# The last projection of a gated mixer layer by seven products over pairs of chunks

## The chip, the cores and the metric

The kernel runs on one core of a Trainium2 chip. The metric is the time of one execution on the device in microseconds (us). A time from a profile belongs to one profiled execution, in which every instruction has a start and a duration. The engines have these names: PE is TensorE (its weight loads are listed apart as PEld), DVE is VectorE, ACT is ScalarE, POOL is GpSimd, and SP is SyncE, which issues the DMA transfers here. PE writes its sums to PSUM, where DVE and ACT read them; everything else lies in SBUF or in the chip's memory.

## What is computed

One layer of a streaming encoder, in f32, with a sequence of 2048 rows and 1024 channels:

```python
h = rms_norm(x, norm_g[l]) * (1.0 + scale) + shift
u = h @ w_in[l]
glu_in, gate_a, q, k, v, gate_b, m_a, m_b = jnp.split(u, IN_SPLITS, axis=-1)
y_a = conformer_conv_branch(glu_in, gate_a, w_dw[l], b_dw[l], ln_g[l], ln_b[l], w_conv_out[l])
...
o = stick_breaking_attention(q, k, v).reshape(bsz, seq, D_SB)
y_b = (o * jax.nn.silu(gate_b)) @ w_sb_out[l]
y = jax.nn.sigmoid(m_a) * y_a + jax.nn.sigmoid(m_b) * y_b
x = x + gate * (y @ w_out[l])
```

The convolution branch is a gated linear unit, a causal depthwise convolution of width 31 and a layer norm. The change concerns the last line, `y @ w_out`, a product of 2048 x 1024 by 1024 x 1024.

## The kernel before

The arrays lie transposed, with 128 channels on the partitions. The sequence is cut into four chunks of 512 rows (`CH`, `NCH`), and a matrix with 1024 channels into eight tiles of 128 x 512 (`KC` = 8; `JC` = 4 for the 512 channels of a branch). Every f32 operand is split in two: `hi` is a rounded copy (by ACT's cast, L102) and `lo` is what is left of it (a subtraction, L103). A product of f32 quality is then three matmuls into one PSUM tile, hi·hi, hi·lo and lo·hi (`mm3`, L135); all matmuls are recorded under L115, so groups are told apart by the names of their tiles. `dense` (L140) runs `mm3` over eight blocks of channels: 24 matmuls of 128x512 for one output tile.

The stages follow one another:

- To 167 us: modulation vectors, the norm, `h` in all four chunks, and the first group of q.
- To about 620 us, the **convolution stage**. Its code runs through blocks one after another: `glu(j)` (L645; two pieces of weights, B and A), `silu_block` (the gates `ga` and `gb`), `qk_group` and `v_block` (two pieces each). A **piece** is a 128x1024 block of weights, loaded by `piece(src)` in two halves: SP loads a half into a tile `wl` (two buffers), ACT casts it to `whi`, POOL subtracts to get `wlo`. The pieces rotate through three slots, two in the pool `wpa` and one in `wpb`, which every third piece takes. Most blocks are four groups of 24 matmuls. Beside them DVE runs the taps of the convolution (L620), which `tick()` hands out at a fixed rate, and reads the sums of PE out of PSUM (five buffers). ACT computes sigmoids and squares. POOL does little but L103.
- To about 790 us: the layer norm of the convolution branch, with group 5 of v and some gates as matmuls beside it. It begins when the convolution's results (`cv`) are stored and read back.
- To about 1540 us: attention by heads, with the matmuls of the merge gates `ma` and `mb` as filler.
- The **last stage**: for each chunk, `y_tiles` (L1036) forms eight tiles of `y` from the branches' operands `za` (convolution) and `zb` (attention output times its gate, which POOL multiplies at L1030), and then `out_tile` (L1065) forms eight tiles of the projection. The results of `y_tiles` are split into `yh` (ACT, L1061) and `yl` (DVE, L1062). The output weights `wo0` to `wo7` are loaded and split once at the start of this stage and stay; `wo0` lies in the left pool `wr`, the others in the right pool `wor`. One output tile is evicted by one DVE instruction (L1073), gate times sum plus x, and stored.

Each engine works through its instructions in a fixed order. In the convolution stage the order is that of the code (the pin at the stage's start), with the taps put late by a priority; in the last stage it comes from the program's order and from when tiles come free. SP issues loads and stores in one order, too, so that a load can stand behind a store that waits for its data.

The core of the last stage:

```python
for ch in range(NCH):
    ...
    for _ in ygen:
        pass
    if ch + 1 < NCH:
        za = load_za(ch + 1)
        zb = load_zb(ch + 1)
    for j in range(KC):
        ...
        out_tile(ch, j, y, psum)
```

## Time and profile before

| what | us |
|---|---|
| runs | 1875.19 (median), 1873.1, 1876.87 |
| the profiled execution | 1877.81 |
| its span, first to last instruction | 1876.1 |
| PE busy in the span | 1797.0 |
| last matmul starts | 1871.44 |

The page gives each engine's busy time, the span in 40 slices (each 46.9 us; a digit is the busy share in tenths) and the chain of work that ended last, followed back from the end. A row of a group reads: line, engine, operation, output<-inputs, shape and count, then busy time, mean of one in ns, and the idle time of the engine just before them with what ended it. A row of windows reads: stretch, its length, the busy time of PE, PEld, DVE, ACT and POOL with counts, then the granted clock of PE, the busy share of the DMA engines, and GB/s.

### The profile page before, as it was taken

The page shows a single profiled execution, that of the slowest core. Times are in us where ns is not written, and L with a number is a line of the kernel's source. Part 1 is how long each engine was busy: PE and PEld are TensorE (multiplying, and loading weights), DVE is VectorE, ACT ScalarE, POOL GpSimd, SP SyncE. Part 2 cuts the span into 40 slices and gives each one's busy share as a digit, 9 for nine tenths or more (in the row PEclk, how much of TensorE's full clock was granted, in tenths as well). Part 3 has the DMA queues.
Part 4 walks back from the last instruction along what each step waited for, and adds up shares of the span by engine and source line. Part 5 has one row for each costly group of instructions (what it writes and reads, how often), then busy time and mean ns, then how long its engine had stood idle before and what let it go on. Part 6 is the DMA issues. An engine that isn't in the chain of part 4 may idle for free.

```text
span 1876.1 us, 27226 instructions
## 1 busy us (share of the span) xinstructions
PE 1797.0 (96%) x9612; PEld 1517.0 (81%) x9612; DVE 1228.2 (65%) x1696; ACT 812.8 (43%) x1880; POOL 681.3 (36%) x899
## 2 busy tenths in 40 slices
PE   6899999999999998999999999999999899999999
PEld 5888889899888977778877778777788677888887
DVE  7646578888879354467777777777777895334341
ACT  5465113232231122267766777776777752010110
POOL 0343111111121143466666666666666641010100
PEclk9999999999999999999999999999999999999999
DMA  8553402325132443432232323132322446353532
GB/s 288 169 186 105 137 29 80 90 67 148 45 104 93 157 141 118 149 128 81 79 96 68 102 63 109 61 93 70 99 65 88 131 143 215 107 163 96 164 95 79
DMA packets 117596, 211.08 MB, mean 113 GB/s; under 512 B 15442, under 2 KB 27730, under 8 KB 117460
## 3 DMA queue, kind: packets, MB, share of 16 engines
q1 hardware_dynamic: 116308, 207.24, 35.5%
q10 hardware_dynamic: 1152, 2.10, 0.3%
q8 instruction: 76, 1.25, 0.3%
q14 instruction: 60, 0.49, 0.1%
HBM read 137.98 MB, written 71.30 MB: 112 GB/s over the span
## 4 chain that ended last, share of the span: by engine, by line
PE 72%; DVE 8%; POOL 6%; issue 5%; DMA 5%; ACT 4%; SPq 1%; DVEq 0%; ACTq 0%; POOLq 0%
PE pd L115 38%; PE po L115 9%; PE p L115 8%; PE av L115 5%; PE pT L120 5%; PE z L115 5%; POOL w L952 3%; DVE sc L945 2%; POOL wlo L103 1%; ACT z L941 1%; DMA xt<-in_x_n_dram 1%; PE pt L120 1%; DVE tlo L979 1%; DMA wa<-in_w_ada_dram 1%; DMA gt<-ga 1%
## 5 line engine op out<-in xcount | busy, mean ns | idle before, releaser
L952 POOL TENSOR_TENSOR w<-w,sc 128x512 f32<-128x512 f32 (+1 forms) x320 | 361.6, 1130 | 251.8 <-DVE sc L945 179.1
L115 PE MATMUL pd<-hhi,whi 128*128 128x512 f32 x1024 | 413.4, 404 | 1.0 <-ACT vsg L858 1.0
L115 PE MATMUL pd<-hhi,wlo 128*128 128x512 f32 x1024 | 402.7, 393 | 0.0
L115 PE MATMUL pd<-hlo,whi 128*128 128x512 f32 x1024 | 402.5, 393 | 0.0
L945 DVE TENSOR_TENSOR_SCAN sc<-z,sc,w 128x512 f32<-128x512 f32 x192 | 245.0, 1280 | 90.9 <-ACT z L941 83.6
L103 POOL TENSOR_TENSOR wlo<-wl,whi 128x512 fp32r<-128x512 f32 x88 | 131.3, 1503 | 401.4 <-ACT whi L102 401.2
L115 PEld LDWEIGHTS pd<-hhi,wlo 128*128 128x128 f32 x1024 | 193.5, 189 | 42.5 <-POOL wlo L103 0.2
L940 ACT ACTIVATE w<-z 128x512 f32<-128x512 f32 (+1 forms) x320 | 172.2, 538 | 125.7 <-PE z L115 100.0
L115 PEld LDWEIGHTS pd<-hhi,whi 128*128 128x128 f32 x1024 | 195.5, 191 | 35.4 <-ACT vsg L858 1.4
L115 PEld LDWEIGHTS pd<-hlo,whi 128*128 128x128 f32 x1024 | 194.3, 190 | 34.3
L979 DVE TENSOR_TENSOR tlo<-pT,thi 128x512 fp32r<-128x512 f32 (+1 forms) x320 | 184.2, 598 | 35.8 <-ACT thi L978 32.4
L115 PE MATMUL z<-kt,q 128*128 128x512 f32 (+2 forms) x640 | 192.7, 382 | 5.0 <-DVE sc L945 3.5
L978 ACT CAST thi<-pT 128x512 fp32r<-128x512 f32 (+1 forms) x320 | 165.4, 527 | 61.3 <-PE pT L120 57.4
L120 PE MATMUL pT<-ident,w 128*128 128x128 f32 x1088 | 173.1, 275 | 9.8 <-POOL w L952 9.5
L120 PEld LDWEIGHTS pT<-ident,w 128*128 128x128 f32 x1088 | 137.5, 141 | 45.9 <-POOL w L952 14.5
L115 PE MATMUL pd<-whi,hhi 128*128 128x256 f32 x608 | 169.7, 287 | 3.6 <-ACT hhi L131 1.9
L941 ACT ACTIVATE z<-z 128x512 f32<-128x512 f32 (+1 forms) x320 | 171.7, 537 | 0.0
L115 PE MATMUL pd<-whi,hlo 128*128 128x256 f32 x608 | 167.0, 285 | 2.3 <-DVE hlo L131 1.7
L115 PE MATMUL pd<-wlo,hhi 128*128 128x256 f32 x608 | 154.0, 284 | 0.0
L949 DVE TENSOR_TENSOR_SCAN sc<-z,tri 128x512 f32<-128x512 f32 (+3 forms) x128 | 104.4, 819 | 53.9 <-ACT z L941 41.9
L115 PE MATMUL av<-tlo,vt 128*128 128x512 f32 (+1 forms) x320 | 123.2, 385 | 14.0 <-DVE tlo L979 10.9
L115 PEld LDWEIGHTS z<-kt,q 128*128 128x128 f32 x640 | 109.6, 189 | 24.1 <-DVE sc L945 5.4
(284 smaller groups left out, 3108.4 us busy)
## 6 DMA issues: line engine op xcount, KB each, us to landing
wl<-in_w_in_dram SPq DMA_DIRECT2D x64, 256.0 KB, 2.9
wa<-in_w_ada_dram SPq DMA_DIRECT2D x24, 512.0 KB, 5.1
wl<-in_w_qkv_dram SPq DMA_DIRECT2D x36, 256.0 KB, 2.7
xt<-in_x_n_dram SPq DMA_DIRECT2D x16, 512.0 KB, 5.5
vst<-st SPq DMA_DIRECT2D x64, 128.0 KB, 2.0
kt<-kst SPq DMA_DIRECT2D x32, 256.0 KB, 2.8
vt<-vst SPq DMA_DIRECT2D x32, 256.0 KB, 2.7
q<-qst SPq DMA_DIRECT2D x32, 256.0 KB, 2.8
```

Of the source, the lines that this page charges most:

```text
L103: (lo_eng or nc.gpsimd).tensor_tensor(out=lo[:, s], in0=wl, in1=f(hi[:, s]), op=ALU.subtract)
L115: i = nc.tensor.matmul(*a, **k)
L120: i = nc.tensor.transpose(*a)
L940: nc.scalar.activation(out=w[:, lo:], in_=z[:, lo:], func=AF.Sigmoid, scale=HD ** -0.5)
L941: nc.scalar.activation(out=z[:, lo:], in_=z[:, lo:], func=AF.Sigmoid, scale=-HD ** -0.5)
L945: nc.vector.tensor_tensor_scan(out=s[:, 1:], data0=z, data1=w, initial=s[:, 0:1], op0=ALU.mult, op1=ALU.bypass)
L949: nc.vector.tensor_tensor_scan(out=s[:, lo + 1:], data0=z[:, lo:], data1=tri[:, :CH - lo], initial=1.0, op0=ALU.mult, op1=ALU.max)
L952: nc.gpsimd.tensor_tensor(out=w[:, lo:], in0=w[:, lo:], in1=s[:, lo:CH], op=ALU.mult)
L978: nc.scalar.copy(out=thi[:, :n], in_=pT[:, :n])
L979: nc.vector.tensor_tensor(out=tlo[:, :n], in0=pT[:, :n], in1=f(thi[:, :n]), op=ALU.subtract)
```

## The change

Two chunks are taken together. With y cut in two halves of channels and two chunks, and `w_out` in two by two halves, the projection of a pair is a product of 2 x 2 blocks, which Strassen's method forms with seven block products instead of eight; each has weights A, operands B and one or more outputs, which are sums and differences of blocks. The table `SEVEN` lists for each product its terms of A, of B and its outputs as (row, column, sign), in the order in which they run: 2, 4, 1, 6, 3, 7, 5. A block product is 4 output tiles of 4 blocks of channels, 48 matmuls; there are 14 in all.

- **The weights' sums.** `prepare()` stands in the convolution stage behind each `piece` of `glu` and `silu_block`, 14 times. Each call makes two of the 28 sums (seven products by four j): loads of one or two 128x512 blocks into `wl`, POOL's addition where there are two terms, the cast, POOL's subtraction, and two stores to the chip's memory (`ws`). It takes a slot of `wpa` or `wpb` and counts as a piece in their rotation. Products 2, 1, 6, 7 and 5 have two terms, 4 and 3 one.
- **The products.** `operands` loads the four weights of a product (512 KB each) and forms its B: POOL's sum where there are two terms, ACT's cast, DVE's subtraction. It is called one product ahead. `product` runs the matmuls, and DVE adds each PSUM tile, times gate or minus gate, to one or two accumulators per output tile (`acc`, twelve buffers, loaded with x); the last addition is followed by the store. The operands go by turns to tiles `za`, `zb` and `oa`, `ob`; `ob` lies in the right pool `yr`, the other three left.
- **The order.** The y tiles of chunks 0 and 1 run one after the other, then seven products, then the y tiles of chunks 2 and 3, then seven products. y stays in f32, so the split behind `y_tiles` goes, and so do the resident output weights. The buffers of `io` go from four to eight.

```diff
+    SEVEN = {
+        2: (((1, 0, 1), (1, 1, 1)), ((0, 0, 1),), ((1, 0, 1), (1, 1, -1))),
+        4: (((1, 1, 1),), ((1, 0, 1), (0, 0, -1)), ((0, 0, 1), (1, 0, 1))),
+        1: (((0, 0, 1), (1, 1, 1)), ((0, 0, 1), (1, 1, 1)), ((0, 0, 1), (1, 1, 1))),
...
+        5: (((0, 0, 1), (0, 1, 1)), ((1, 1, 1),), ((0, 0, -1), (0, 1, 1))),
+    }
+    LASTS = {(1, 0): 4, (1, 1): 3, (0, 0): 5, (0, 1): 5}
+    H = KC // 2
...
+        def prepare():
+
+            npiece[0] += 1
+            pool = wpb if npiece[0] % 3 == 0 else wpa
+            hi = pool.tile([P, 1024], F32R, tag="whi", name="whi")
+            lo = pool.tile([P, 1024], F32R, tag="wlo", name="wlo")
+            for i in range(2):
+                m, j = wanted.pop(0)
+                s = slice(i * CH, (i + 1) * CH)
+                w = []
+                for r, c_, _ in SEVEN[m][0]:
+                    w.append(wpa.tile([P, CH], F32, tag="wl", name="wl", bufs=2))
+                    nc.sync.dma_start(w[-1], w_out[j + H * r][:, c_ * CH:(c_ + 1) * CH])
+                if len(w) == 2:
+                    nc.gpsimd.tensor_tensor(
+                        out=w[0], in0=w[0], in1=w[1],
+                        op=ALU.add if SEVEN[m][0][1][2] > 0 else ALU.subtract)
+                nc.scalar.copy(out=hi[:, s], in_=w[0])
+                nc.gpsimd.tensor_tensor(out=lo[:, s], in0=w[0], in1=f(hi[:, s]),
+                                        op=ALU.subtract)
+                ws_d[m, j] = dram(f"ws{m}_{j}", [P, 2, CH], F32)
+                nc.sync.dma_start(ws_d[m, j][:, 0, :], f(hi[:, s]))
+                nc.sync.dma_start(ws_d[m, j][:, 1, :], f(lo[:, s]))
...
                 w = piece(w_in[B_GLU_B + j])
+                prepare()
                 for g in ORDER:
...
-            return yp.tile([P, CH], F32, tag="io", name=name, bufs=4)
+            return yp.tile([P, CH], F32, tag="io", name=name, bufs=8)
...
+        def operand(q, half, i):
+
+            pool = yr if (q, half) == ("o", "b") else yp
+            return pool.tile([P, 2, CH], F32R, tag=f"{q}{half}{i}", name=f"{q}{half}{i}")
...
-                nc.vector.tensor_tensor(out=ma, in0=ma, in1=mb, op=ALU.add)
-                hi = yp.tile([P, CH], F32R, tag=f"yh{j}", name=f"yh{j}")
-                lo = yp.tile([P, CH], F32R, tag=f"yl{j}", name=f"yl{j}")
-                nc.scalar.copy(out=hi, in_=ma)
-                nc.vector.tensor_tensor(out=lo, in0=ma, in1=f(hi), op=ALU.subtract)
...
+                y[ch, j] = (yr if ch % 2 else yp).tile([P, CH], F32, tag=f"y{j}", name=f"y{j}")
+                nc.vector.tensor_tensor(out=y[ch, j], in0=ma, in1=mb, op=ALU.add)
                 yield
...
+        def operands(m, ch):
+
+            q = "zo"[turn[0] % 2]
+            turn[0] += 1
+            A, B = [], []
+            for j in range(H):
+                A.append(operand(q, "a", j))
+                nc.sync.dma_start(f(A[j]), ws_d[m, j])
+            for kc in range(H):
+                B.append(operand(q, "b", kc))
+                t = combined(SEVEN[m][1], lambda t: y[ch + t[1], kc + H * t[0]],
+                             lambda: yp.tile([P, CH], F32, tag="io", name="sum", bufs=8),
+                             nc.gpsimd)
+                nc.scalar.copy(out=B[kc][:, 0, :], in_=t)
+                nc.vector.tensor_tensor(out=B[kc][:, 1, :], in0=t, in1=f(B[kc][:, 0, :]),
+                                        op=ALU.subtract)
+            return A, B
...
+        def product(m, ch, A, B, psum):
+            for j in range(H):
+                ps = psum("po")
+                for kc in range(H):
+                    s = slice(kc * P, (kc + 1) * P)
+                    mm3(ps, A[j][:, 0, s], A[j][:, 1, s], B[kc][:, 0, :], B[kc][:, 1, :],
+                        kc == 0, kc == H - 1)
+                for r, c_, sign in SEVEN[m][2]:
...
+                    nc.vector.scalar_tensor_tensor(
+                        out=o, in0=ps, scalar=(gate if sign > 0 else ngate)[:, row:row + 1],
+                        in1=o, op0=ALU.mult, op1=ALU.add)
+                    if LASTS[r, c_] == m:
+                        nc.sync.dma_start(out_t[row][:, ts_], o)
...
+        za, zb = load_za(1), load_zb(1)
+        steps(ygen)
+        steps(y_tiles(1, za, zb, psum, y))
+        ya = s3.enter_context(tc.tile_pool(name="ya", reuse_waits="tile", bufs=1, side="right"))
+        for ch in (0, 2):
             if ch:
...
+                za3, zb3 = load_za(3), load_zb(3)
+                steps(y_tiles(2, za, zb, psum, y))
+                steps(y_tiles(3, za3, zb3, psum, y))
+            order = list(SEVEN)
+            nxt = operands(order[0], ch)
+            for i, m in enumerate(order):
+                A, B = nxt
+                if i + 1 < len(order):
+                    nxt = operands(order[i + 1], ch)
+                elif ch == 0:
+                    za, zb = load_za(2), load_zb(2)
+                product(m, ch, A, B, psum)
```

Two places show how the instructions move. The first is POOL in the convolution stage, from the second piece of `glu(2)` to the two pieces of `qk_group(2)` and of `v_block(4)`. Before, only the real pieces' subtractions stand there (two per piece; the numbers tell the pieces apart):

```order
L103 TENSOR_TENSOR wlo_3866<-wl_3867,whi_3865 128x512
L103 TENSOR_TENSOR wlo_3866<-wl_3871,whi_3865 128x512
L103 TENSOR_TENSOR wlo_3992<-wl_3993,whi_3991 128x512
L103 TENSOR_TENSOR wlo_3992<-wl_3997,whi_3991 128x512
L103 TENSOR_TENSOR wlo_4002<-wl_4003,whi_4001 128x512
L103 TENSOR_TENSOR wlo_4002<-wl_4007,whi_4001 128x512
```

After the change, on the same engine at the same place, with the additions of `prepare` at L234 and its subtractions at L238:

```order
L103 TENSOR_TENSOR wlo_4008<-wl_4009,whi_4007 128x512
L103 TENSOR_TENSOR wlo_4008<-wl_4013,whi_4007 128x512
L234 TENSOR_TENSOR wl_4019<-wl_4019,wl_4021 128x512
L238 TENSOR_TENSOR wlo_4018<-wl_4019,whi_4017 128x512
L234 TENSOR_TENSOR wl_4029<-wl_4029,wl_4031 128x512
L238 TENSOR_TENSOR wlo_4018<-wl_4029,whi_4017 128x512
L103 TENSOR_TENSOR wlo_4156<-wl_4157,whi_4155 128x512
L103 TENSOR_TENSOR wlo_4156<-wl_4161,whi_4155 128x512
L103 TENSOR_TENSOR wlo_4166<-wl_4167,whi_4165 128x512
L103 TENSOR_TENSOR wlo_4166<-wl_4171,whi_4165 128x512
```

Four POOL instructions, each pair behind loads of its own, now stand ahead of the two pieces 4156 and 4166 of `qk_group(2)`.

The second place is DVE where y tiles begin behind a projection. Before, at the end of chunk 1's projection and the start of chunk 2's y tiles, the splits of the next operands (L1010) stand ahead of most of the projection's evictions (L1073):

```order
L1010 TENSOR_TENSOR zb_17167<-o,zb_17167 128x512
L1010 TENSOR_TENSOR zb_17175<-o,zb_17175 128x512
L1073 SCALAR_TENSOR_TENSOR xt<-po,gate,xt 128x512
L1010 TENSOR_TENSOR zb_17183<-o,zb_17183 128x512
L1073 SCALAR_TENSOR_TENSOR xt<-po,gate,xt 128x512 x7
L1056 TENSOR_TENSOR ma<-p_17427,ma 128x512
```

After, where the seventh product of the first pair ends (evictions at L1160) and chunk 2's y tiles begin (their first reading of PSUM at L1108); `za_177..` and `zb_177..` are operands of chunk 3:

```order
L1057 TENSOR_TENSOR za_17770<-n,za_17770 128x512
L1057 TENSOR_TENSOR zb_17780<-o,zb_17780 128x512
L1057 TENSOR_TENSOR zb_17788<-o,zb_17788 128x512
L1160 SCALAR_TENSOR_TENSOR acc<-po,ngate,acc 128x512
L1160 SCALAR_TENSOR_TENSOR acc<-po,gate,acc 128x512
L1057 TENSOR_TENSOR za_17775<-n,za_17775 128x512
L1057 TENSOR_TENSOR zb_17796<-o,zb_17796 128x512
L1057 TENSOR_TENSOR zb_17804<-o,zb_17804 128x512
L1108 TENSOR_TENSOR ma<-p_17816,ma 128x512
L1109 TENSOR_TENSOR mb<-p_17829,mb 128x512
```

Three splits of chunk 3 now stand between the last eviction of the product and the first of chunk 2's y tiles, where nothing stood between projection and y tiles before.

More of the change, by code (lines that the diff above doesn't have):

```diff
@@ L1014, in load_za @@
             for kc in range(JC):
-                t = yp.tile([P, 2, CH], F32R, tag=f"za{kc}", name=f"za{kc}")
+                t = operand("zooz"[ch], "a", kc)
                 o = io("n")
@@ L1024, in load_zb @@
             for kc in range(JC):
-                t = yp.tile([P, 2, CH], F32R, tag=f"zb{kc}", name=f"zb{kc}")
+                t = operand("zooz"[ch], "b", kc)
                 o = io("o")
@@ new lines, in y_tiles, with combined @@
+                nc.vector.tensor_tensor(out=y[ch, j], in0=ma, in1=mb, op=ALU.add)
+                yield
+        def combined(terms, part, tmp, eng):
+            if len(terms) == 1:
+                return part(terms[0])
+            t = tmp()
+            (a, b) = terms
+            eng.tensor_tensor(out=t, in0=part(a), in1=part(b),
+                              op=ALU.add if b[2] > 0 else ALU.subtract)
+            return t
+        turn = [0]
+        def operands(m, ch):
[14 more added lines that the diff above has]
+            return A, B
```

50 lines of the change are left out of this document (22 added, 28 removed), and 3 rows, old and new, of the table SEVEN.

## The prediction

> **What bounds the kernel now.** I read the page first (busy shares, slices, the chain's shares), then the chain of waits in order of time, then windows by stage.
>
> ```profile
> PE 1797.0 (96%) x9612; PEld 1517.0 (81%) x9612; DVE 1228.2 (65%) x1696; ACT 812.8 (43%) x1880; POOL 681.3 (36%) x899
> DVE  7646578888879354467777777777777895334341
> PE 72%; DVE 8%; POOL 6%; issue 5%; DMA 5%; ACT 4%; SPq 1%; DVEq 0%; ACTq 0%; POOLq 0%
> ```
>
> TensorE is busy 96% of the span and holds 72% of the chain. The VectorE slices fall to 1 to 4 tenths in the last eighth, so an added operation is cheap there, and stand at 7 and 8 in slices 4 to 12, where the weights are to be prepared.
>
> ```profile
> 167.87 5.47 PE pd L115 x24
> ...
> 191.51 115.86 PE pd L115 x624
> ...
> 621.34 2.51 POOL wlo L103 x2
> ...
> 1567.41 39.93 PE po L115 x170
> 1607.33 43.52 PE p L115 x192
> 1650.86 44.64 PE po L115 x192
> ...
> 1827.19 44.66 PE po L115 x192
> ```
>
> Start, length and count of pieces of the chain. From 191 us the convolution stage is pure TensorE; its first gap is at 621. The tail alternates y tiles (`p`) and output projection (`po`) with nothing between. So a matmul removed from the tail is time, and so is any gap added to the convolution stage: a late piece of weights has no cover.
>
> **Tail: the matmuls.** 4 x 8 x 8 x 3 = 768 become 2 x 7 x 4 x 4 x 3 = 672.
>
> ```profile
> L115 PE MATMUL po<-yh,wo7l 128*128 128x512 f32 x32 | 12.7, 396 | 0.0
> L115 PE MATMUL po<-yh,wo0l 128*128 128x512 f32 x32 | 12.5, 390 | 0.0
> L115 PE MATMUL p<-za,wc2l 128*128 128x512 f32 x16 | 6.3, 391 | 0.0
> ```
>
> A `po` piece takes 44.64/192 = 0.2325 us per matmul, a `p` piece 43.52/192 = 0.2267. The modelled means say which operand matters: wo0, in the left pool as the y weights are, reads like `p` (390 ns), wo7 in the right pool 396. The products' weights all lie in the left pool, but in every second product the moving operand `ob` lies right, where no row shows it. Four pieces make 178.6 us; 672 matmuls cost 152.3 at 0.2267, 156.2 at 0.2325. Gain 22.4 to 26.3; I take the middle, **-24.5**, as half the operands are of the unseen kind.
>
> **Tail: the other engines.**
>
> ```profile
> L1073 DVE SCALAR_TENSOR_TENSOR xt<-po,gate,xt 128x512 f32<-128x512 f32 x32 | 23.7, 750 | 100.2 <-PE po L115 92.0 <-DMA xt<-in_x_t_dram 8.2
> L1062 DVE TENSOR_TENSOR yl<-ma,yh 128x512 fp32r<-128x512 f32 x32 | 22.1, 691 | 19.8 <-ACT yh L1061 19.6
> L1030 POOL TENSOR_TENSOR o<-o,gb 128x512 f32<-128x512 f32 x13 | 17.0, 1313 | 201.6 <-DMA gb<-gb 125.5 <-DMA o<-o 76.1
> L1010 DVE TENSOR_TENSOR zb<-o,zb 128x512 fp32r<-128x512 f32 x13 | 13.9, 1067 | 20.9 <-ACT zb L1009 20.4
> ```
>
> 96 evictions replace 32: 64 x 0.75 = 48 us of VectorE; 56 splits replace 32: 24 x 0.69 = 17. A product of 48 matmuls (10.9 us) holds about 7 evictions (5.2) and 4 splits (2.8), so VectorE fits, and so do 4 POOL sums of 1.31. Cost 0 inside the products. At the end two evictions stand behind the last matmul where one stood: **+0.75**.
>
> ```profile
> 1565.15 0.39 PE L115 MATMUL po<-yh,wo0l 128*128 128x512 f32 x1
> 1566.60 0.51 PE L115 MATMUL po<-yh,wo0h 128*128 128x512 f32 x1 [1.06 <-ACT yh L1061]
> 1567.41 0.50 PE L115 MATMUL po<-yl,wo0h 128*128 128x512 f32 x1 [0.30 <-DVE yl L1062]
> ```
>
> These gaps (starts 1.45 and 0.81 apart instead of 0.225) are waits for the y split, which goes: **-1.8**. In its place chunk 1's y tiles stand directly behind chunk 0's, and wait for their gated attention operand: load, POOL product, cast, split. One such chain is 2.7 + 1.31 + 0.62 + 1.07 = 5.7 us; bounds 0 and 5.7, and I take what the gap there is today, **+1.8**. At chunk 2, VectorE has chunk 3's splits (za, zb) ahead of chunk 2's first evictions, as the rows of the change show; while they wait for loads, evictions and with them PSUM stand still. Bounds 0 and one chain again: **+3**.
>
> ```profile
> 1566.00:1571.00 5.00, 4.10 (x16) 3.11 (x17) 3.19 (x5) 2.93 (x6) 0.00 (x0) 1.00 0.95 311
> ```
>
> Transfers in the first pair's products: 28 weight loads of 512 KB, 16 x_t loads, 16 stores, 12 z loads of 256 KB are 26 MB, of which some 5 are issued ahead: 21 MB in 76 us is 280 GB/s. This window moved 311 at a DMA share of 0.95, so it fits, tightly. Bounds 0 and 8 (26 MB at 311 GB/s take 84 us): **+1**.
>
> **Convolution stage: what the preparation costs.** Each of 14 calls adds two sums behind a piece of weights; 10 calls have two terms in each sum, 4 have one. All go through the same two `wl` buffers and three piece slots as the real pieces, and through POOL in program order.
>
> ```profile
> L102 ACT CAST whi<-wl x48: 607/620/657, 166.0 to 599.9; 128x512 fp32r<-128x512 f32 x48
> L103 POOL TENSOR_TENSOR wlo<-wl,whi x48: 1285/1307/2336, 166.7 to 600.8; 128x512 fp32r<-128x512 f32 x48
> ...
> DMA to landing us min/median/max: 2.5/2.7/4.3
> ...
> L103 POOL TENSOR_TENSOR wlo<-wl,whi 128x512 fp32r<-128x512 f32 x49 | 80.6, 1658 | 365.7 <-ACT whi L102 365.5
> ```
>
> The first three are the tile `wl` from 160 to 620 us (ns, min/median/max), the last the group's mean there. A POOL pass takes p = 1.31 us alone and up to 2.34; the mean, 1.66, is what I use.
>
> ```profile
> 599.59 3.53 POOL L103 TENSOR_TENSOR wlo<-wl,whi 128x512 fp32r<-128x512 f32 x2 [18.22 <-ACT whi L102]
> ...
> 600.65 1.32 DVE L620 SCALAR_TENSOR_TENSOR cc<-v,wsum,cc 128x1024 f32<-128x1024 f32 x1
> 601.89 2.31 DVE L620 SCALAR_TENSOR_TENSOR cb<-u,wdw,cb 128x1024 f32<-128x1024 f32 x1
> ...
> 336.00:358.00 22.00, 22.00 (x101) 18.23 (x100) 22.00 (x19) 5.67 (x7) 3.88 (x2) 1.00 0.35 96
> ```
>
> Two passes beside convolution taps take 3.53 together and the tap among them 2.31 where the one before took 1.32: they take turns. In the window 336 to 358 VectorE is busy all 22 us.
>
> The chain for a sum of two terms is load 2.7, add p, cast 0.62, subtract p: 3.32 + 2p = 6.6. Two sums, then the real piece (load, cast, two subtractions; its first load is partly under the sum before): 9.96 + 6p = 19.9, against a block of 4 x 5.47 = 21.9. So a call is hidden behind its block on the mean, with 2 us to spare; scatter of p up to 2.34 costs some. Seven calls stand so: 7 x 0.5 = **+3.5** (0 at p = 1.31; 7 x 1.9 = 13 at 2.3).
>
> Three calls (before qk1, qk2 and v5) stand ahead of **two** pieces, which are used at once, 1.4 us apart: 13.28 + 8p = 26.6 against 23.3, 3.3 late each: **+9.8** (1.4 at 1.31, 25 at 2.3). The second piece of a pair now takes the slot that the block just before it frees; cast and subtraction behind that are within these 3.3.
>
> What the added waits hold up: on SP a sum's two stores wait for its POOL subtraction, and behind them stand the next `wl` loads, which is in the chain above, and stores of gate and q tiles, at most one sum late. On ScalarE 28 casts (17 us) wait for loads ahead of the sigmoids that free PSUM; ScalarE is busy 5.67 of 22 us in the window above and five PSUM buffers stand ahead: 0, and up to one chain of 6.6 if PSUM fills. The 27 MB of added loads and stores in 450 us are 60 GB/s beside 96 at a share of 0.35: 0.
>
> ```profile
> 666.53 1.39 PE L115 MATMUL psb<-dg,ones 128*128 128x128 f32 x8 [2.38 <-DVE dg L755]
> ...
> 667.25:670.66 3.41, 3.41 (x11) 2.78 (x10) 2.80 (x5) 0.98 (x2) 1.91 (x3) 0.50 0.45 148
> ```
>
> After an idle time of 2.38 us the granted clock was 0.50 for 3.41 us: half of those, 1.7, were lost. Stalls of 3.3 would do the same: 3 x 1.7 = **+5.1** (0 to 5.1). [...]
>
> Removed from the attention stage's end: 16 casts, 16 VectorE subtractions and 16 loads of the output weights; there TensorE was the bound and they cost nothing, nor does their going gain.
>
> **Sum** against the profiled execution (1877.81; span 1876.1, and 1.7 around it): -24.5 + 0.75 - 1.8 + 1.8 + 3 + 1 + 3.5 + 9.8 + 5.1 = -1.35. The profiled run lies 2.6 above the median of the runs; carried to that, 1875.19 - 1.35 = 1873.8.
>
> **Rivals.**
> *The preparation is hidden.* With p near its median 1.31 the pairs lose 1.4, the rest and the clock nothing: 17 less, about **1856.8**. For it: the median, and stretches such as 415 to 460 in which taps pause. Against it: POOL passes come in rows here, and the second of a row pays.
>
> *POOL and the taps take turns, slower than before.* Added POOL passes make rows of four to eight behind each other while taps stream. At p = 2.1 the pairs cost 20.3, the seven others 4.6, the clock 5.1: 30.0 instead of 18.4, **1885.4**; at 2.3, 1898. It decides from p = 1.72 (no gain) and from 1.87 (slower by 0.2%). For it: the 3.53 us pair and VectorE's full windows; delayed taps also come late at 620, where the LN stage waits. Against it: TensorE's own stalls give VectorE time to pause. [...]
>
> *Transfers bind the products.* 26 MB at 311 GB/s with nothing ahead: +8 instead of +1, **1880.8**. Against it: the weights are loaded one product early.
>
> **How the numbers follow.** Forecast (pieces late before the pairs) 0.38; hidden 0.30; turns 0.24; transfers 0.08. About 0.2% (3.75 us) is what a measurement of this kernel can tell from no change. The forecast's case spreads over 1865 to 1881: faster 0.12, same 0.20, slower 0.06. Hidden: faster 0.29, same 0.01. Turns: slower 0.23, same 0.01. Transfers: slower 0.05, same 0.03. Together faster 0.41, same 0.25, slower 0.34. The range reaches from just below the hidden case, 1855, to p = 2.2, 1893. The likeliest case's own range is 1865 to 1881.
>
> **What would show it.** The products: 14 pieces of 48 matmuls of 10.9 to 11.2 us, without gaps but for those at chunk 2's start. In the convolution stage: TensorE idle before the second piece of qk1, qk2 and v5, released by POOL's subtraction, each with a half-clock window behind it; POOL's mean between 1.5 and 1.8. A mean below 1.4 and a gap-free stage make the first rival right; above 1.9, the second. A DMA share over 0.95 through the products with TensorE waiting for `za` or `oa` is the third. I am wrong altogether if gaps appear in the attention stage, which the change does not touch.

## The result, and the profile after

The changed kernel takes 1886.56 us (median of 1885.76 to 1887.02), the kernel before 1874.14 (1872.94 to 1876.87) beside it: ratio 1.0064, interval 1.0046 to 1.0081. It is slower by 0.6%. The forecast was 1873.8, no change that can be measured.

The page of the changed kernel, the rows that answer to those of before (busy shares, VectorE's slices, the chain's shares):

```profile
PE 1779.0 (94%) x9516; PEld 1503.8 (80%) x9516; DVE 1319.4 (70%) x1769; ACT 836.2 (44%) x1916; POOL 815.5 (43%) x987
DVE  7645598798888654448777777777777787576475
PE 54%; DVE 14%; DMA 10%; POOL 8%; issue 7%; ACT 5%; SPq 2%; DVEq 0%; ACTq 0%; POOLq 0%
```

TensorE is busy 18 us less, about what 96 matmuls fewer should make it, yet its share of the chain falls from 72% to 54%: VectorE, DMA, POOL and the rest have taken it. VectorE's slices 6 to 13 read 7 to 9 before and after, so the page alone does not show what changed there.

Where the time went can be counted by matching the matmuls of the two traces, which run in the same order from 167 us to the end of attention. The shift is the start in the changed kernel's profiled execution less that in the one before; starts come from the two timelines.

| matmul | start before | shift | step |
|---|---|---|---|
| second piece of qk1, lo part | 281.05 | +1.9 | +1.7 |
| second piece of qk2, lo part | 383.66 | +3.7 | +1.7 |
| transposes at the end of qk2 | 422.21 | +9.0 | +4.6 |
| behind them, at a granted clock of 0.50 | 424.43 | +11.1 | +2.1 |
| first matmul of v5 | 622.54 | +25.3 | +14.0 |
| first matmuls of attention | 803.51 | +26.6 | +1.3 |
| last matmul of attention | 1540.05 | +30.9 | +4.3 |
| end of the span | 1876.1 | +7.8 | -23.1 |

The step is the jump at that matmul; behind qk2 and in the last three rows it is the growth since the row above. Steps under 1 us are left out. So the convolution stage cost 26.6 us instead of 18.4. The new last stage gave 23.1, but 4.3 were lost at the end of attention just before it; together that is 18.8, close to what was forecast. (The medians differ by 12.4, more than these 7.8: the profiled execution of before was 3.7 above its median, that of the changed kernel 0.8 below. In two later kernels with the same layer norm stage it came out 1.5 and 3.1 us shorter than in that profile.)

The step of 14.0 us is one wait, in the timeline of PE in the changed kernel and, for comparison, in the kernel before:

```profile
647.82 0.58 PE L115 MATMUL pd<-whi,hhi 128*128 128x256 f32 x1 [15.77 <-DVE sg L726]
```

```profile
622.54 0.38 PE L115 MATMUL pd<-whi,hhi 128*128 128x256 f32 x1 [1.75 <-DVE sg L679]
```

What is waited for is no piece of weights. It is the product of the last gate tile of `gb` (L726, L679 before), the last instruction that reads a PSUM buffer of the convolution stage: v5 opens another PSUM pool in the same space, and its first matmul waits until the old one is empty. Before, five PSUM buffers let TensorE run ahead of the readers, and only 1.75 us showed; all lateness that has gathered by then comes due at this place.

How it gathered shows in two places. The first is ScalarE's order (ACT in the changed kernel):

```profile
593.92 0.62 ACT L237 CAST whi<-wl 128x512 fp32r<-128x512 f32 x1 [6.25 <-POOL wl L234]
594.45 0.59 ACT L725 ACTIVATE sg<-pd 128x512 f32<-128x512 f32 x1
601.90 0.62 ACT L237 CAST whi<-wl 128x512 fp32r<-128x512 f32 x1 [6.86 <-POOL wl L234]
604.75 0.62 ACT L102 CAST whi<-wl 128x512 fp32r<-128x512 f32 x1 [2.23 <-DMA wl<-in_w_in_dram]
605.28 0.59 ACT L725 ACTIVATE sg<-pd 128x512 f32<-128x512 f32 x1
```

The casts of two sums and of a piece stand ahead of these two sigmoids, and they wait for POOL's additions and for a load. Before, the same two sigmoids started at 577.71 and 582.95, so they are 16.7 and 22.3 us late. TensorE itself is 11.3 us late by then; some 11 of the 14 us have thus gathered by 605.28, while these two sigmoids have no wait of their own.

The second place is the chain of waits a little later, in order of time (start, length, what; a piece that begins with DMA ends at landing):

```profile
610.21 2.53 DMA wl<-in_w_out_dram
...
612.90 1.44 POOL wl L234
614.36 0.33 SPq L232
...
614.74 3.19 DMA gb<-sg
...
618.04 0.61 ACT sg L725
618.67 0.69 DVE sg L726
619.36 2.12 DVE cc L664
...
630.05 1.52 POOL wlo L238
631.58 0.33 SPq L242
...
632.00 2.48 DMA gb<-sg
...
640.54 2.28 DVE cc L674
642.82 0.61 DVE sg L726
643.45 2.88 DMA gb<-sg
...
646.44 0.61 ACT sg L725
```

The chain runs through both kinds of work by turns. A gate tile's store (`gb<-sg`) is issued at 614.74 only when SP has issued the load ahead of it, and that load waited for POOL's addition to give up a `wl` tile; at 632.00 the store stands behind the store of a sum (L242) that waits for POOL's subtraction. The next sigmoid waits for this store to land, because `sg` is a single tile. VectorE's product stands behind taps of 2.1 and 2.3 us. Sigmoid, product, store, sigmoid is a loop, and where it becomes longer than the 5.47 us in which TensorE makes a group, the tiles can't catch up: the last sigmoid, at 646.44, is 25.3 us later than before.

The waits of the sigmoids show it (engine, line, what ended the wait: total us, times, longest), first the changed kernel, then the one before:

```profile
ACT sg L725 <- DMA gb<-sg: 22.3, 6, 7.0
ACT sg L725 <- PE pd L115: 0.5, 1, 0.5
```

```profile
ACT sg L678 <- PE pd L115: 33.1, 7, 4.8
ACT sg L678 <- DMA gb<-sg: 4.3, 1, 4.3
```

Before, the sigmoids waited mostly for TensorE, as they should; now their own waits are for stores. (The waits of the casts ahead of them are not counted here.)

The other large step, 4.6 us at the end of qk2, is VectorE's alone:

```profile
431.20 1.07 PE L120 MATMUL pt<-ident,qn 128*128 128x128 f32 x3 [4.39 <-DVE qn L342]
```

The normalized tile `qn` stands in VectorE's order behind the taps of a convolution, and the last operation of that convolution ended at 426.8 instead of 410.3. The groups of taps, changed kernel and before (busy us, mean ns):

```profile
L664 DVE SCALAR_TENSOR_TENSOR cc<-v,wsum,cc 128x1024 f32<-128x1024 f32 x56 | 92.2, 1647 | 0.0
L664 DVE SCALAR_TENSOR_TENSOR ca<-u,wdw,ca 128x1025 f32<-128x1025 f32 x60 | 87.8, 1464 | 0.0
L664 DVE SCALAR_TENSOR_TENSOR cb<-u,wdw,cb 128x1024 f32<-128x1024 f32 x56 | 86.9, 1552 | 0.0
```

```profile
L620 DVE SCALAR_TENSOR_TENSOR ca<-u,wdw,ca 128x1025 f32<-128x1025 f32 x60 | 80.4, 1341 | 0.0
L620 DVE SCALAR_TENSOR_TENSOR cc<-v,wsum,cc 128x1024 f32<-128x1024 f32 x56 | 79.4, 1417 | 0.0
L620 DVE SCALAR_TENSOR_TENSOR cb<-u,wdw,cb 128x1024 f32<-128x1024 f32 x56 | 78.6, 1404 | 0.0
```

Together 266.9 instead of 238.4 us. With the stage's other operations of that kind, the trace before has 18 over 1.9 us among 184, the trace after 46.

POOL's own passes are no worse than forecast:

```profile
L238 POOL TENSOR_TENSOR wlo<-wl,whi 128x512 fp32r<-128x512 f32 x28 | 41.7, 1493 | 110.3 <-ACT whi L237 110.2
L234 POOL TENSOR_TENSOR wl<-wl 128x512 f32<-128x512 f32 x20 | 31.1, 1554 | 82.9 <-DMA wl<-in_w_out_dram 82.9
```

The last stage, in windows (PE, PEld, DVE, ACT, POOL busy; clock, DMA share, GB/s) and PE's timeline:

```profile
1636.00:1712.00 76.00, 76.00 (x336) 62.72 (x335) 61.72 (x82) 20.29 (x33) 25.09 (x19) 1.00 0.79 278
1712.00:1725.00 13.00, 12.07 (x52) 9.37 (x50) 6.25 (x9) 3.01 (x5) 5.23 (x4) 1.00 0.96 338
```

```profile
1725.31 0.73 PE L115 MATMUL p<-oa,wc2h 128*128 128x512 f32 x2 [1.23 <-DVE ma L1108]
```

The first seven products run without a gap (76.00 of 76) beside 278 GB/s; VectorE is busy 62 of 76 us. One wait of 1.23 us follows where chunk 2's y tiles begin.

The 4.3 us at the end of attention have one large wait among them (PE's timeline, then pieces of the chain of waits):

```profile
1522.69 1.22 PE L115 MATMUL z<-kt,q 128*128 128x512 f32 x2 [5.05 <-DVE sc L992]
```

```profile
1518.45 1.23 POOL o L1082
...
1519.71 0.63 ACT zb L1056
...
1520.36 1.09 DVE zb L1057
1521.45 1.21 DVE sc L992
```

Attention's scan (`sc`) stands in VectorE's order behind the split of an operand of the y tiles (`zb`), which waits for the cast and that for POOL's product. The same matmul waited 1.29 us before. The kernel without the preparation, below, has this wait too (5.02 us), so it comes with the new last stage; which of its edits brings it, the eight buffers of `io` for instance, was not tested.

### The profile page after: what moved, and what is told of

Its sections match the earlier page's. It is cut to its first block, busy times and chain, and to the rows that moved or that the text cites. A ratio compares the mean times of both kernels' runs of the same rounds, so it can differ in the third digit from the quotient of the medians.

```text
span 1883.9 us, 27529 instructions
## 1 busy us (share of the span) xinstructions
PE 1779.0 (94%) x9516; PEld 1503.8 (80%) x9516; DVE 1319.4 (70%) x1769; ACT 836.2 (44%) x1916; POOL 815.5 (43%) x987
## 3 DMA queue, kind: packets, MB, share of 16 engines
q8 instruction: 75, 1.23, 0.3%
## 4 chain that ended last, share of the span: by engine, by line
PE 54%; DVE 14%; DMA 10%; POOL 8%; issue 7%; ACT 5%; SPq 2%; DVEq 0%; ACTq 0%; POOLq 0%
PE pd L115 24%; PE p L115 8%; PE po L115 7%; PE av L115 5%; PE pT L120 5%; PE z L115 5%; POOL w L999 3%; DVE sc L992 2%; POOL wlo L103 2%; DVE cc L664 2%; DMA wl<-in_w_out_dram 1%; DVE ca L664 1%; DVE cb L664 1%; DVE tlo L1026 1%; DMA wl<-in_w_qkv_dram 1%
## 5 line engine op out<-in xcount | busy, mean ns | idle before, releaser
L103 POOL TENSOR_TENSOR wlo<-wl,whi 128x512 fp32r<-128x512 f32 x88 | 137.4, 1572 | 150.5 <-ACT whi L102 138.4
L115 PEld LDWEIGHTS pd<-whi,hhi 128*128 128x128 f32 x608 | 118.9, 196 | 18.5 <-DVE sg L726 16.2
```

The costliest lines, as they stand in the source:

```text
L103: (lo_eng or nc.gpsimd).tensor_tensor(out=lo[:, s], in0=wl, in1=f(hi[:, s]), op=ALU.subtract)
L115: i = nc.tensor.matmul(*a, **k)
```

## The experiments

Two theories stood against each other. **A**: POOL's passes and VectorE's taps take turns, and what VectorE reads late holds up TensorE. **B**: SP's queue and the single `sg` hold up the gate tiles. The forecast's own idea, that weight pieces come late, is the third. Where no interval is given, a time is that of one execution; those of the kernel before lie between 1870.8 and 1879.3 us, so differences of a few us say little. The gap before v5 of 16.2 us in the expectations is counted between the starts of two matmuls; the rows count the idle time, 15.77.

**The last stage alone** (`e1_tail_only`):

```diff
         def prepare():
+            if len(wanted) < 28:
+                return
...
-                nc.sync.dma_start(f(A[j]), ws_d[m, j])
+                nc.sync.dma_start(f(A[j]), ws_d[2, 0])
```

> Only the first of the 14 preparations is left; all products load that one sum as their weights, so the output is not the layer's. This is the changed last stage alone. If the last stage gains what the prediction says (19.8 us) and the convolution stage holds the whole loss, the time is 1853 to 1857 us and TensorE has no gap over 3 us before 622 us. If part of the loss sits in the new last stage, the time is above 1860.

1854.0 us beside 1876.08: -22.1. The last matmuls of the convolution stage start 1.5 us earlier than in the profile of before (618.92 instead of 620.40) and the first of attention 3.0; the other 20.8 us of the span (1852.3 instead of 1876.1) come behind that, from the last stage and the end of attention. TensorE has no gap over 3 us before 622, as expected. The whole loss lies in the preparation, 32.6 us between this kernel and the changed one.

**No POOL passes** (`e2_no_pool`):

```diff
-                if len(w) == 2:
-                    nc.gpsimd.tensor_tensor(
...
-                nc.gpsimd.tensor_tensor(out=lo[:, s], in0=w[0], in1=f(hi[:, s]),
-                                        op=ALU.subtract)
+                nc.scalar.copy(out=lo[:, s], in_=w[-1])
```

> All loads, casts and stores of the preparation stay; its 48 POOL passes are left out (two casts of the loaded blocks take their place), so the output is not the layer's. Theory A (POOL passes and VectorE's convolution taps take turns, so evictions come late): the gap before v5 (16.2 us in the changed kernel) falls below 6 and the time to 1857 to 1866. Theory B (stores of gate tiles stand behind loads in SP's queue and the single tile sg holds up the next sigmoid): the loads and stores are all there, the gap stays above 8 and the time above 1872.

1859.35 us, within A's range. The gap before v5 is almost that of the kernel before, and the one at the end of qk2 is gone:

```profile
623.96 0.39 PE L115 MATMUL pd<-whi,hhi 128*128 128x256 f32 x1 [2.27 <-DVE sg L721]
```

The steps of 1.6 and 2.4 us at the second pieces of qk1 and qk2 stay, though no sum needs POOL. They come from the slots: in the changed kernel the casts of the second piece of qk1 start at 278.70, when ScalarE has been idle for 9.75 us and TensorE has left the slot.

**No transfers** (`e3_no_dma`):

```diff
                 for r, c_, _ in SEVEN[m][0]:
+                    if len(wanted) < 26:
+                        w.append(fx[0])
+                        continue
                     w.append(wpa.tile([P, CH], F32, tag="wl", name="wl", bufs=2))
...
+                if len(wanted) < 26:
+                    continue
                 ws_d[m, j] = dram(f"ws{m}_{j}", [P, 2, CH], F32)
```

> The reverse: behind the first call the preparation's POOL passes and casts run on a constant tile, its loads and stores are left out, so the output is not the layer's. Theory A: the gap before v5 stays above 8 us, the time is 1872 to 1887. Theory B: the gap falls below 6 and the time to 1855 to 1866.

1866.04 us, and

```profile
629.45 0.58 PE L115 MATMUL pd<-whi,hhi 128*128 128x256 f32 x1 [5.01 <-DVE sg L737]
```

The gap is below B's bound of 6 and the time at the end of B's range (1866), while the run without POOL passes spoke for A. Against the last stage alone, the transfers and casts cost 5.4 us (no POOL), POOL and casts 12.0 (no transfers), and all together 32.6. So the two are not rivals: nearly half of the loss (15.2 us) arises only where they meet. The waits of 1.43 us at the second pieces of qk1 and qk2 stay here too.

**Two buffers for sg** (`e4_sg2`), the changed kernel otherwise:

```diff
-                    sg = cvp.tile([P, CH], F32, tag="sg", name="sg", bufs=1)
+                    sg = cvp.tile([P, CH], F32, tag="sg", name="sg", bufs=2)
```

> The changed kernel with two buffers for sg instead of one: a sigmoid no longer waits for the store of the gate tile before. Theory B: the gap before v5 falls from 16.2 us to below 6, the time to 1872 to 1877. Theory A: the evictions are late by VectorE, the gap stays above 12, the time is 1883 to 1887.

1874.3 us, 12 less than the changed kernel's median. The gap before v5 falls as B says, to just above its bound; the one at the end of qk2 is unchanged (4.7 us between starts), as A asks. The sigmoid that started at 605.28 starts at 605.42 here, as late as before the edit, but the last one at 634.88 instead of 646.44: the second buffer does not keep the gate tiles from coming late, it lets them catch up. The gap before v5 is now:

```profile
639.15 0.58 PE L115 MATMUL pd<-whi,hhi 128*128 128x256 f32 x1 [6.21 <-DVE sg L726]
```

**The passes on VectorE** (`e5_dve`):

```diff
-                    nc.gpsimd.tensor_tensor(
+                    nc.vector.tensor_tensor(
                         out=w[0], in0=w[0], in1=w[1],
...
-                nc.gpsimd.tensor_tensor(out=lo[:, s], in0=w[0], in1=f(hi[:, s]),
+                nc.vector.tensor_tensor(out=lo[:, s], in0=w[0], in1=f(hi[:, s]),
```

> The 48 passes of the preparation run on VectorE (0.69 us each, 33 us in all) instead of POOL; nothing else changes. In the changed kernel the taps took 28.5 us more in sum. If it is VectorE's load that makes the evictions late, whichever way it comes about, this is no better: gap before v5 12 us or more, time 1882 to 1892. If it is the long single taps and the slow passes in a row (theory A in the narrow sense), VectorE's order with short passes is better: gap 4 to 10, time 1868 to 1880.

1865.79 us, 21 less than the changed kernel, below even the range of the narrow theory A. The passes themselves (group rows):

```profile
L238 DVE TENSOR_TENSOR wlo<-wl,whi 128x512 fp32r<-128x512 f32 x28 | 19.0, 686 | 8.3 <-ACT whi L237 8.2
L234 DVE TENSOR_TENSOR wl<-wl 128x512 f32<-128x512 f32 x20 | 13.8, 688 | 19.3 <-DMA wl<-in_w_out_dram 18.7 <-issue 0.6
```

32.8 us of VectorE; of the 184 operations of the taps' kind, which were 285 us long in the changed kernel, 18 are over 1.9 us and the sum is 256. VectorE thus works as long as in the changed kernel (289 against 285), in shorter pieces. v5 begins without a wait; a gap of 3.11 us follows at its second piece (631.38), released by that piece's cast (`ACT whi L102`) and not by a gate tile.

**Both** (`e6_dve_sg2`, and once more with five rounds as `e6b_dve_sg2`); the edit is that of the two before together.

> Passes on VectorE and two buffers for sg. If the two causes add up in one loop (sigmoid, product behind taps, store in SP's queue), taking both away leaves the two gaps of 1.7 us at the second pieces of qk1 and qk2 and little else: 1858 to 1868. If VectorE's load alone decides, 1872 to 1882, with the gap at the end of qk2 (4.7 us) still there.

> The kernel with the passes on VectorE and two buffers for sg once more, for an interval. One look gave 1857.16 against 1874.89 before, of which some 3 us may be the layer norm stage, which comes out 3 us shorter or longer from run to run of other kernels. 1855 to 1861, ratio 0.989 to 0.993.

1857.16 us in one run, then 1860.49 (1859.67 to 1863.34) beside 1874.70, ratio **0.9927, interval 0.9913 to 0.9942**. TensorE has no gap over 1 us before v5 any more; left are those at the second pieces of qk1 and qk2 (1.8 and 2.0 us between starts, 1.49 and 1.70 idle). This version beats both kernels.

**The preparation in attention** (`e7_attn`), POOL's passes kept:

```diff
+                            if g % 2 == 1 and wanted and i:
+                                prepare(2 if (i, g) in FIRST else 1)
                             if g == 0 and i + 1 < len(rest):
                                 nxt = load_piece(wpa, w_in[rest[i + 1][0]])
```

> The 28 sums are prepared in the attention stage (one or two behind every second group of the merge gates' matmuls, in the tiles of the next piece), none in the convolution stage, whose piece rotation is that of the kernel before. The last stage alone gave 1854.0. If the cost of the preparation lies in where it stands, the convolution stage loses nothing and attention 0 to 10 us: 1854 to 1866, 0.6 to 1.1% faster than before. If POOL's 48 passes cost VectorE's time wherever they stand, attention loses 15 to 30: 1869 to 1884.

1891.42 us, ratio 1.0089 (1.0057 to 1.0121), slower than either bound. The convolution stage is that of before to within 1 us (first attention matmuls 2 us earlier); the windows over attention, before and here:

```profile
832.00:1560.00 728.00, 698.96 (x3626) 568.37 (x3625) 552.60 (x706) 510.79 (x1064) 454.08 (x703) 1.00 0.30 92
```

```profile
832.00:1560.00 728.00, 676.54 (x3454) 545.97 (x3453) 523.78 (x660) 505.38 (x1059) 505.24 (x741) 0.98 0.39 123
```

POOL does 51 us more, TensorE 22 less and at a clock of 0.98. The first product begins 36 us later than in the last stage alone. POOL's multiplications stand between attention's scans and transposes. That the added passes are paid for this reason is argued, not shown: their loads, casts and stores were added with them.

**The kernel before with two buffers for sg** (`e8_before_sg2`), a control:

> The kernel before with two buffers for sg, a control. If the second buffer helps only where stores of gate tiles come late, as in the changed kernel, nothing changes: within 2 us of the kernel before. If it gains by itself, 1866 to 1872, and the gain of 12 us that it gave the changed kernel says little on the preparation.

1872.46 us beside 1874.89 (1871.56 to 1878.10): 0.4 us more than the 2 that were expected, but within the spread. The convolution stage is the same to 1 us, and the layer norm stage 3.1 us shorter. The second buffer helps where stores come late.

**The calls ahead of qk1 and qk2 moved to v4** (`e9_best`, on top of e6):

```diff
                 w = piece(w_in[B_GLU_A + j])
-                prepare()
+                if j not in (1, 2):
+                    prepare()
...
                 w2 = [piece(w_qkv[grp, i]) for i in range(2)]
+                prepare()
+                prepare()
```

> As that, and the two preparations that stood ahead of qk1 and qk2 are moved behind the pieces of v group 4. If the gaps of 1.8 to 2.0 us at the second piece of qk1 and of qk2 come from the slots' rotation (the second piece waits for the block just before to end), both go and the time is 1853 to 1857, 2 to 4 us below the kernel beside it. If they come from VectorE or SP being behind, they stay or move to v group 4 or glu 3, and the time is within 2 us.

1872.62 us, ratio 0.9988 (0.9977 to 0.9999), a miss. Both gaps at the second pieces went, as the slots' rotation asks, but a new one came:

```profile
466.46 0.80 PE L115 MATMUL pd<-hhi,whi 128*128 128x512 f32 x1 [12.51 <-ACT whi L102]
```

The second call waits for a slot until v4's block ends (its cast comes at 452.61), and the pieces of glu 3 stand behind it. This is the forecast's mechanism, late pieces, at its largest.

**No slot for a preparation** (`e10_noslot`): hi and lo are formed within the two `wl` tiles, and the moved calls stand in v4 and qk3.

```diff
+                w = [wpa.tile([P, CH], F32, tag="wl", name="wl", bufs=2) for _ in range(2)]
...
+                nc.scalar.copy(out=w[1].bitcast(F32R), in_=w[0])
+                nc.vector.tensor_tensor(out=w[0].bitcast(F32R), in0=w[0], in1=w[1],
+                                        op=ALU.subtract)
```

> Passes on VectorE, two buffers for sg, and the sums are formed within the two wl tiles, so that a preparation takes no slot and the pieces rotate as in the kernel before; the calls ahead of qk1 and qk2 stand behind the pieces of v group 4 and of qk3 instead, one each. If the slots are what costs the gaps of 1.8 to 2.0 us at the second pieces (and the 12.8 us before glu 3 in the kernel that moved the calls without freeing the slots), all of them go: 1853 to 1858. If the two wl tiles, held until the stores land, now delay the pieces, gaps appear at other blocks and the time is 1860 or more.

1877.37 us, ratio 1.0015 (1.0004 to 1.0026), a miss. The second pieces are on time, but other blocks wait, and before v5:

```profile
638.34 0.58 PE L115 MATMUL pd<-whi,hhi 128*128 128x256 f32 x1 [9.23 <-DVE sg L723]
```

Casts of sums make sigmoids late here as well (they wait 8.25, 7.93, 6.30 and 7.08 us for the addition), but with two buffers for sg the gate tiles catch up: the last sigmoid but one, at 628.94, waits for TensorE again. What v5 waits for is VectorE's order, in which the last operations of a convolution stand ahead of the last two products (the last operation and the two products):

```profile
634.80 2.28 DVE L670 TENSOR_TENSOR cc<-cc,ca 128x1024 f32<-128x1024 f32 x1
637.01 1.27 DVE L723 TENSOR_TENSOR sg<-pd,sg 128x512 f32<-128x512 f32 x2
```

**Twice the passes on VectorE** (`e11_dve_twice`, one buffer for sg):

```diff
+                for _ in range(3 if len(w) == 2 else 2):
+                    nc.vector.tensor_tensor(out=lo[:, s], in0=w[0], in1=f(hi[:, s]),
+                                            op=ALU.subtract)
```

> The passes run on VectorE as in the kernel that gave 1865.8, and each sum's subtraction is repeated so that there are 96 passes of 0.69 us instead of 48: 33 us more of VectorE in the convolution stage, so that its load (taps and passes, 322 us) is far above that of the changed kernel (285). If the load of VectorE makes the gate tiles late, this is as slow as the changed kernel or slower: 1882 or more. If it is POOL's passes beside taps (46 taps over 1.9 us against 18), the time stays near the single version: 1866 to 1875.

1897.4 us, the time that a theory of load expects, but not by its way: v5 begins without a wait, and its second piece comes 2.49 us late, released by a cast of weights, as are gaps at other blocks (2.71 us at 624.90):

```profile
654.32 0.58 PE L115 MATMUL pd<-whi,hhi 128*128 128x256 f32 x1 [2.49 <-ACT whi L102]
```

The doubled passes lengthen the preparation's own chain, so pieces come late. More load on VectorE costs much, then, and a wait for `qn` at the end of qk2 is there again (3.62 us), but the long wait for gate tiles is not.

## Why the prediction was wrong

**The step that failed** is the one that costed the added waits: "On ScalarE 28 casts (17 us) wait for loads ahead of the sigmoids that free PSUM; ScalarE is busy 5.67 of 22 us in the window above and five PSUM buffers stand ahead: 0, and up to one chain of 6.6 if PSUM fills." The waits for readers of PSUM measured 4.6 + 14.0 = 18.6 us. The step asked whether ScalarE has time, and not what stands ahead of a sigmoid in its order: casts that waited 6.25, 6.86 and 2.23 us stood ahead of two sigmoids in a row, and 11 of the 14.0 us had gathered there. Beside it stands the sentence on SP, that "stores of gate and q tiles" come "at most one sum late". That is about right for one store (the one ready at 611.99, when the product ended, was issued at 614.74), but `sg` is one tile, so each late store delays the next sigmoid, and the lateness of one group is handed to the next: sixteen gate tiles run on end from ga2 to gb1, and the last sigmoid came at 646.44, 25.3 us later than before (621.17; 11.3 of them are TensorE's own shift). A bound of one chain was set where chains add up. The 4.6 us at the end of qk2 are another omission: taps that the added passes made longer stood ahead of `qn` on VectorE, which has no term in the sum. (The wait is gone in the run without POOL passes, and stays with two buffers for sg.) The kernel before showed the place: its 1.75 us before v5 is a wait for the same product, and the prediction quoted the POOL subtraction next to it in the chain and did not ask PE's own timeline who released it.

Point by point, in us:

| term | forecast | measured |
|---|---|---|
| seven single calls | +3.5 | about 1 (drift up to 281 us) |
| three pairs of pieces | +9.8 | +3.4 (qk1, qk2; v5's wait was another) |
| half clock | +5.1 | +3.4 (2.1 behind qk2, 1.3 behind v5) |
| readers of PSUM late | 0 | +18.6 |
| matmuls of the products | -24.5 | -25.9 (14 x 10.91 = 152.7 instead of 178.6) |
| gaps behind the split of y | -1.8 | -1.9 |
| start of chunk 1's y tiles | +1.8 | 0 |
| start of chunk 2's y tiles | +3 | +1.4 |
| y tiles with `oa` and `ob` | 0 | +2.6 |
| end of attention | 0 | +4.3 |
| transfers beside the products | +1 | 0 |
| end | +0.75 | about +0.5 |

- *The last stage* was right in its sum (-19.75 forecast with the gap of 1.8 that goes; -18.8 measured and, with nothing prepared, -20.8), but in part by luck, since costs that were not forecast stood against gains that were larger than forecast. All products ran at 0.227 us per matmul, those with `ob` in the right pool too, so the pool of the moving operand did not matter there. The y tiles of chunks 1 and 2, whose operands lie in `oa` and `ob`, ran at 0.2333, those of chunks 0 and 3, in `za` and `zb`, at 0.2267: some 2.6 us, and no run shows why. Transfers of 278 GB/s were forecast as 280 and did not bind. Also not forecast were the 4.3 us at the end of attention. The prediction names gaps in the attention stage, "which the change does not touch", as a sign of being wrong altogether; one of 5.05 us is there, behind operands of the y tiles that are formed in that stage, so the change reached it after all.
- *Late pieces* were over-priced: 3.3 us each for the pairs before qk1 and qk2 was 1.7. The runs without POOL passes and without transfers keep such steps, the moved calls make them vanish, and the casts there wait for TensorE, so they are waits for a slot, which the forecast called part of the 3.3. The chain of sums, which the forecast took for the cause, was not the bound there. The four calls with one term, put at nothing without a reason, show no step over 1 us.
- *POOL's passes* at 1.66 us were right (1.49 and 1.55 for the new, over 1.7 for L103). That they would lengthen taps was seen in one pair of rows and charged to POOL only; VectorE's share, 28.5 us over the stage, was not in the sum.
- *The rival that POOL and the taps take turns* named the direction and, with 1885.4, nearly the time, the latter by luck: its point of decision was wrong, as it asked for p above 1.72, and the new passes stayed below. It should have been priced on VectorE's side. The trace has single taps at 2.1 to 2.3 instead of 1.28 us, but only 46 of the 184 operations of the taps' kind took over 1.9 us, and p's mean did not go to 2.3. (The prediction's slices of 7 and 8 tenths on VectorE are 6 to 13, not 4 to 12; no term rests on them.)
- *The clock*: the price of 1.7 us for a window at half clock was about right (behind qk2 TensorE was busy 4.73 us at a granted clock of 0.50, 429.10 to 435.93, and lost 2.1; behind v5 the clock was 0.50 from 647.82 to 650.97, and 1.3 were lost), but the waits that were to cause it were shorter. One of 1.44 us (qk1) was followed by a granted clock of 1.00; in the one of 4.39 us (qk2) it fell to 0.50. In the kernel with the passes on VectorE a wait of 1.70 us at qk1 was followed by 0.50, as its windows before and behind it show:

```profile
278.90:281.47 2.57, 0.87 (x6) 0.67 (x6) 2.57 (x2) 0.04 (x1) 1.94 (x1) 1.00 0.35 102
281.47:284.88 3.41, 3.41 (x18) 3.41 (x17) 3.41 (x3) 1.20 (x2) 2.74 (x2) 0.50 0.26 77
```

A wait of that length was not always followed by half clock: behind the 1.75 us before v5 in the kernel before (622.54) the granted clock was 1.00. The last section counts such stretches in two traces.

**What is shown and what is open.** Shown: the preparation alone carries the loss; POOL's passes cost 27 us of it beside the transfers (changed kernel against no POOL passes) and, with the casts, 12 without them; a second `sg` takes 12 away, and passes on VectorE 21. That most of the lateness before v5 gathers behind casts that wait on ScalarE, and that one `sg` keeps the gate tiles from catching up, is read from the traces of the changed kernel and of that with two buffers; no run moves the casts alone. Open: why passes on VectorE, with the same total work on that engine, are so much better. Shorter waits of the casts for the additions (57.6 us in all instead of 78.3), shorter single taps in front of each gate product, and shorter waits of SP all fit; no run here keeps one and takes away the others.

## What to carry to other kernels

A bound that holds for one late store doesn't hold for a loop through a single buffer: before putting work beside a stage that is all TensorE, look at what stands ahead of each reader of PSUM in its engine's order and how long that can wait, follow the reader round its loop (sigmoid, product, store, sigmoid), and compare the loop, with the longest instruction that can stand in front at each step, with the time in which TensorE makes a group. Look at the small gaps that such a stage already has and ask the engine's own timeline who released them: at the change of a PSUM pool all lateness comes due (15.77 us of idle time before v5 here). Elementwise passes are not free because "an idle engine" takes them: POOL was busy 79.55 of 460 us in the convolution stage of the kernel before (160 to 620 us), and beside 48 more passes there, in the changed kernel, the groups of taps took 266.9 instead of 238.4 us on VectorE. And one SP queue ties transfers together that have nothing to do with each other: here the store of a gate tile, ready at 611.99, was issued at 614.74, behind a load for a sum.

## What the runs showed of the hardware

- Two buffers for the gate tile were worth 12 us in the changed kernel (1874.3 instead of 1886.56), and nothing that can be told from the spread in the kernel before (1872.46 beside 1874.89).
- A 128x512 f32 pass took 0.69 us on VectorE and 1.49 to 1.55 on POOL beside taps; moving 48 of them to VectorE, which looked the busier engine of the two, took 21 us off.
- In attention the same 48 passes on POOL (with their transfers) cost some 36 us, although POOL was busy 454 of 728 us there before.
- In the traces of the kernel before and of the changed kernel the stretches at half clock (granted clock 0.50) begin whole multiples of 3.41 us apart, as at 667.25, 694.56 and 735.52 in the kernel before (8 and 12 times 3.41). With the time from 180 to 1000 us cut into such windows, a window at full clock with over 1.9 us of idle TensorE was followed by one at half clock 7 times out of 7, one with 1.7 to 1.9 us 0 times out of 2 (in the kernel with the passes on VectorE, above, a wait of 1.70 us was followed by half clock), and one with 1.0 to 1.7 us 0 times out of 7. The length of a gap alone did not decide: 2.38 us in one window were followed by half clock (666.53, the kernel before), 2.28 us of which 1.12 lay in one window and 1.16 in the next were not (693.09, the changed kernel).
- Matmuls of y tiles with moving operands in `oa` and `ob` ran at 0.2333 us each, with `za` and `zb` at 0.2267; in the products there was no such difference (0.227).
